# Gated FFN up-projection: the two products that need only token chunk 0 computed ahead of the seven-product loop, and no tile computed classically any more

## The chip, the cores and the metric

One NeuronCore of a Trainium2 chip runs the whole kernel. The metric is the device time of one execution in microseconds (us); the median of several executions is compared. The engines are named as the profile names them: PE (TensorE), PEld (its weight loads), DVE (VectorE), ACT (ScalarE), POOL (GpSimd), SP (SyncE, which issues every DMA here).

## What is computed

Two residual layers over x of shape (1, 1024, 1024) in float32: layer 0 has a mixer of attention and spatial gating, layer 1 a convolution module. After each mixer comes the same gated feed-forward block, and a final norm ends the program. The change touches the feed-forward block only:

```
def conv_ffn(h, w_up, dw_w, dw_b, w_down):
    hh = causal_dwconv(h @ w_up, dw_w, dw_b)      # w_up: 1024 x 5632, conv width 3 along the tokens
    a, gate = jnp.split(hh, 2, axis=-1)           # 2816 channels each
    return (a * jax.nn.silu(gate)) @ w_down

x = x + conv_ffn(rms_norm(x, norm_ffn_g[l]), ffn_w_up[l], ffn_dw_w[l], ffn_dw_b[l], ffn_w_down[l])
```

## The kernel before

**Precision.** Each float32 operand of a matmul is split into a rounded high part and a low rest (`split_hi_lo`: the high part is a cast on ACT, L143, the low part a subtraction on POOL or DVE, L147), and three matmuls replace one (`PASSES`). A matmul here has a 128x128 weight block and 512 columns. The tokens come in two chunks of 512; `hT[0]` and `hT[1]` hold the normalised, transposed and split activations of chunk 0 and 1.

**Up-projection, classical.** The 5632 output channels are 22 gate tiles and 22 value tiles of 128 channels. `head_steps` computes a gate tile and its value tile for one chunk: 2 x 24 matmuls (`chan_mm`, L307), the convolution as one ACT pass (L582) and two DVE passes over 512 columns (L585) with small halo operations (L588, L591), Silu on ACT (L598) and the product on DVE (L602). 3 of the 22 pairs of tiles in layer 0 (`PRE0`) and 8 in layer 1 (`PRE1`) are done so, for chunk 0 and for chunk 1, beside other work that leaves PE gaps: the norms of chunk 1, the depthwise convolution and layer norm of layer 1's mixer, and `combos`.

**Up-projection, seven products.** The other 19 and 14 pairs go through `pair_steps`, a Strassen scheme of Winograd's form: gate and value tile are the two column blocks, the two halves of the 1024 inputs the row blocks, the two chunks the token blocks. Seven products of 12 matmuls (L680) replace eight. Products 1 and 2 use `hT[0]` (chunk 0) alone; 5, 6 and 7 use the combinations T1, T2, T3 (named t or t12 and t3 in the trace) that `combos` makes by loading the normalised rows of both chunks from DRAM (`xnd`, L633), subtracting (L636 to L639) and transposing (L647); 3 and 4 use `hT[1]`, whose lower half `combos` overwrites with a fourth combination. Products 1, 6, 7, 4 accumulate in a PSUM bank A, 5 and 3 in a bank C, 2 in a bank Bk. A is read out three times on the way: after 1 (p1, ACT, L715), after 6 (u2, ACT, L721), after 7 (DVE, L725) and at the end (ACT, L732); C after 5 (p5, ACT, L718) and 3 (DVE, L723); Bk on DVE (L728). The results go to SBUF rows `rg` and `rv_` of 1024 tokens, which the convolution reads in one ACT pass (L686) and two DVE passes (L688) each; L734 multiplies.

The weights of a tile (512 KB each for gate and value) are loaded by SP (L695), and five of their linear combinations are made by L700, L702, L703 (DVE) and L705 (POOL), split by ACT (L143) and by POOL or DVE (L147). In layer 0 the result is split and stored for a classical down-projection (`store_split`). In layer 1 the down-projection has seven products as well, so `finish` combines each couple of pairs j and j + 11 (`sums`: three POOL operations, L554 to L556, one on DVE, L558) and stores them.

**Order.** Program order only sets priorities: a list scheduler orders every engine's queue at build time, and at run time each queue is strictly in order. `interleave(main, shadow, start, end)` spreads one list of steps over another. `keep_in_program_order` (`pin`) holds an instruction at its place. Pools of fixed size limit how far ahead work can run: 4 raw weight tiles (`WRAW`), 8 split halves (`WHL`), 4 rows (`ROWS`), 4 single banks.

Of the kernel before, what the change touches and what calls it, by code (L numbers as in the profile page):

```python
# [58 lines left out]
def trunk_kernel(ctx: ExitStack, tc: tile.TileContext, x, norm_mix_g, norm_ffn_g, ab_w_in, ab_w_out,  # L59
# [515 lines left out]
    def head_steps(l, c, hT, js):  # L575

        dw, halo, w_up = dws[l], halos[l], ffn_w_up[l]

        def up(ct):
            ps = chan_mm(chan_unit(w_up, ct), hT[c])  # L580
            y = s2([P, CH])
            nc.scalar.activation(out=y, in_=ps, func=AF.Identity, scale=dw[:, 2, ct:ct + 1], bias=dw[:, 3, ct:ct + 1])  # L582
            for k in range(2):
                sh = 2 - k
                nc.vector.scalar_tensor_tensor(out=y[:, sh:], in0=ps[:, :CH - sh], scalar=dw[:, k, ct:ct + 1],  # L585
                                               in1=y[:, sh:], op0=ALU.mult, op1=ALU.add)
                if c > 0:
                    nc.vector.scalar_tensor_tensor(out=y[:, :sh], in0=halo[:, ct, k:2], scalar=dw[:, k, ct:ct + 1],  # L588
                                                   in1=y[:, :sh], op0=ALU.mult, op1=ALU.add)
            if c < NCH - 1:  # L590
                nc.vector.tensor_copy(out=halo[:, ct, :], in_=ps[:, CH - 2:])  # L591
            return y

        cur = {}

        def up_g(j):
            cur["g"] = yg = up(HT + j)
            nc.scalar.activation(out=yg, in_=yg, func=AF.Silu)  # L598

        def up_a(j):  # L600
            ya = up(j)
            nc.vector.tensor_tensor(out=ya, in0=ya, in1=cur["g"], op=ALU.mult)  # L602
            if l == 0:
                store_split(ya, s2([P, CH], F32R), j, slice(c * CH, (c + 1) * CH))
            elif c == 0:
                nc.sync.dma_start(out=phs[:, SLOT[1 + j // HH], j % HH, :], in_=ya)
            elif j < HH:
                cur["v"] = ya
            else:
                jj = j - HH  # L610
                old = s4([P, S])
                nc.sync.dma_start(out=old.rearrange("p (i c) -> p i c", i=2), in_=phs[:, 0:3:2, jj, :])
                sums(jj, old[:, :CH], cur["v"], old[:, CH:], ya)
                nc.sync.dma_start(out=phs[:, SLOT[4], jj, :], in_=ya)
                nc.sync.dma_start(out=phs[:, SLOT[7], jj, :], in_=cur["v"])

        return [f for j in js for f in (lambda j=j: up_g(j), lambda j=j: up_a(j))]
# [39 lines left out]
    def pair_steps(l, hT, T, js, up_pool):  # L657
# [12 lines left out]

        def part(raw, lo_eng):
            hl = whl.tile([P, 2, 512], F32R, tag="whl", name="hl")
            split_hi_lo(raw, hl[:, 0, :], hl[:, 1, :], lo_eng=lo_eng)
            return hl.rearrange("p s (d c) -> p s d c", c=P)

        def product(ps, n, hv, start, stop):
            i = 0
            for d in range(4):
                for sw, sa in PASSES:
                    nc.tensor.matmul(ps, lhsT=hv[:, sw, d, :], rhs=B[n](sa, d), start=(start and i == 0),  # L680
                                     stop=(i == 11), skip_group_check=True)
                    i += 1
# [9 lines left out]
        def f(j):  # L692
# [18 lines left out]
            rg, rv_ = row(), row()
            A, C = bank(), bank()
            product(A, 1, a1, True, False)
            p1 = s2([P, CH])
            nc.scalar.copy(out=p1, in_=A)  # L715
            product(C, 5, a5, True, False)
            p5 = s2([P, CH])
            nc.scalar.copy(out=p5, in_=C)  # L718
            product(A, 6, a6, False, False)
# [451 lines left out]
```

## Time and profile before

| | |
|---|---|
| runs | median 2269.41 us of 3 (2268.31 to 2272.55) |
| profiled execution | 2265.38 us, of which the profile's span 2263.6 us |
| PE busy | 2138.7 us, 94% of the span, 9846 matmuls |
| DVE, ACT, POOL busy | 65%, 48%, 40% |
| DMA | 346.58 MB, 16 engines busy 46.3% |

The profile is one execution. Busy time is the union of an engine's instructions; matmuls overlap each other, so the mean duration of one (about 0.39 us) is longer than the distance from one to the next. What a stage costs is read from the distance between equal points of its steps. An idle time and its releaser stand ahead of the instruction that waited.

### The profile page before, as it was taken

To read this page: it belongs to the slowest core of one execution; us is meant where nothing else is said; L and a number is where in the kernel's file an instruction comes from. 1 tells how busy PE (TensorE), PEld (TensorE's weight loads), DVE (VectorE), ACT (ScalarE), POOL (GpSimd) and SP (SyncE) were. 2 spreads that over 40 slices of the span, in tenths; PEclk is the share of its full clock that TensorE was granted. 3 is DMA by queue.
4 is the path that set the end of the run, shared out by engine and by line. 5 is a ranking of instruction groups with operands and counts; after the bars stand their busy time and mean duration, and the time that the engine had idled before them with its cause. 6 is when DMAs were issued, how large, how long until landed. Compare 5 with 4: busy or idle time off the path is not lost. (4 is left out here: it accounts for less than half of the span.)

```text
span 2263.6 us, 28251 instructions
## 1 busy us (share of the span) xinstructions
PE 2138.7 (94%) x9846; PEld 1755.1 (78%) x9846; DVE 1481.1 (65%) x2671; ACT 1092.8 (48%) x1899; POOL 905.1 (40%) x772
## 2 busy tenths in 40 slices
PE   8989999898999999999999979989998999999987
PEld 6768777787788888878788868767777888878876
DVE  5456787458666666600399569996576576756686
ACT  4245665244455555522455474555443454544354
POOL 1222010134344443344489827963544455530011
PEclk9999999999999999999999979989989999999999
DMA  6375433466233333588655723432653223238433
GB/s 226 112 244 172 128 124 134 141 231 197 75 112 105 108 107 109 201 305 286 212 168 168 259 60 100 152 100 93 221 165 127 95 91 117 93 132 319 130 98 107
DMA packets 300495, 346.58 MB, mean 153 GB/s; under 512 B 12988, under 2 KB 207296, under 8 KB 299840
## 3 DMA queue, kind: packets, MB, share of 16 engines
q1 hardware_dynamic: 300352, 344.77, 46.3%
q8 instruction: 78, 1.28, 0.2%
q14 instruction: 65, 0.53, 0.1%
HBM read 261.62 MB, written 83.10 MB: 152 GB/s over the span
## 5 line engine op out<-in xcount | busy, mean ns | idle before, releaser
L147 POOL TENSOR_TENSOR hl<-raw,hl 128x512 fp32r<-128x512 f32 x424 | 570.5, 1364 | 605.4 <-ACT hl L143 511.5
L307 PE MATMUL bank<-big,hl 128*128 128x512 f32 x1824 | 427.7, 394 | 4.1 <-ACT big L223 2.4
L270 PE MATMUL bank<-hl,big 128*128 128x512 f32 x1728 | 422.1, 400 | 7.2 <-ACT big L143 2.8
L143 ACT CAST hl<-raw 128x512 fp32r<-128x512 f32 x476 | 280.0, 618 | 257.5 <-issue 96.9
L307 PEld LDWEIGHTS bank<-big,hl 128*128 128x128 f32 x1824 | 343.2, 189 | 76.6 <-ACT big L223 3.3
L270 PEld LDWEIGHTS bank<-hl,big 128*128 128x128 f32 x1728 | 325.1, 192 | 78.1 <-ACT big L143 3.3
L680 PE MATMUL bank<-big,hl 128*128 128x512 f32 x1584 | 375.3, 390 | 0.3 <-ACT hl L143 0.3
L680 PEld LDWEIGHTS bank<-big,hl 128*128 128x128 f32 x1584 | 297.1, 188 | 64.0 <-ACT hl L143 1.0
L680 PE MATMUL bank<-t,hl 128*128 128x512 f32 x1188 | 290.4, 395 | 6.5 <-ACT hl L143 6.0
L688 DVE SCALAR_TENSOR_TENSOR bank<-row,dw,bank 128x1024 f32<-128x1024 f32 x132 | 169.7, 1286 | 162.8 <-ACT bank L686 161.6
L680 PEld LDWEIGHTS bank<-t,hl 128*128 128x128 f32 x1188 | 224.4, 189 | 57.6 <-ACT hl L143 6.9
L862 PE MATMUL bank<-hl,ph 128*128 128x512 f32 x1056 | 247.9, 395 | 5.3 <-DMA ph<-phd 3.3
L1006 DVE SCALAR_TENSOR_TENSOR sbank<-yb,cw,sbank 128x512 f32<-128x512 f32 x352 | 246.0, 749 | 5.0 <-ACT sbank L995 1.8
L862 PEld LDWEIGHTS bank<-hl,ph 128*128 128x128 f32 x1056 | 199.8, 190 | 49.7 <-DMA ph<-phd 4.3
L824 PE MATMUL bank<-hl 128*128 128x512 f32 x726 | 176.1, 397 | 10.4 <-DVE s L734 4.4
L824 PEld LDWEIGHTS bank<-hl 128*128 128x128 f32 x726 | 138.9, 192 | 42.1 <-ACT hl L143 5.0
L1003 POOL TENSOR_TENSOR ap<-ap,pr 128x512 f32<-128x512 f32 x112 | 147.8, 1319 | 14.2 <-ACT ap L998 10.3
L143 ACT CAST hl<-s 128x512 fp32r<-128x512 f32 x110 | 68.3, 621 | 108.8 <-POOL s L705 50.3
L1002 ACT ACTIVATE pr<-yb,cw 128x512 f32<-128x512 f32 x112 | 80.7, 723 | 63.5 <-POOL ap L1003 62.8
L705 POOL TENSOR_TENSOR s<-raw,s 128x512 f32<-128x512 f32 x33 | 43.6, 1320 | 157.9 <-DVE hl L147 83.5
L1112 POOL TENSOR_TENSOR xr<-xr,gain 128x512 f32<-128x512 f32 x10 | 14.5, 1481 | 201.5 <-ACT xn L1104 176.1
L585 DVE SCALAR_TENSOR_TENSOR s<-bank,dw,s 128x510 f32<-128x510 f32 x88 | 65.5, 745 | 35.8 <-ACT s L582 34.8
(202 smaller groups left out, 2577.3 us busy)
## 6 DMA issues: line engine op xcount, KB each, us to landing
raw<-in_ffn_w_up SPq DMA_DIRECT2D x110, 512.0 KB
ph<-phd SPq DMA_DIRECT2D x88, 512.0 KB
raw<-in_ffn_w_down SPq DMA_DIRECT2D x44, 512.0 KB
phd<-s SPq DMA_DIRECT2D x38, 512.0 KB
ph<-phs SPq DMA_DIRECT2D x33, 512.0 KB
raw<-in_conv_w_in SPq DMA_DIRECT2D x32, 512.0 KB
raw<-in_ab_w_in SPq DMA_DIRECT2D x32, 256.0 KB
qd<-s SPq DMA_DIRECT2D x32, 256.0 KB
```

The source lines that it names most:

```text
L143: nc.scalar.copy(out=hl_hi, in_=raw)
L147: eng.tensor_sub(out=hl_lo, in0=raw, in1=hl_hi.bitcast(F32))
L270: nc.tensor.matmul(ps, lhsT=hT[t // TPC][:, sa, d, tok(t)], rhs=units[d][:, sw, :], start=(n == 0), stop=(n == 3 * DT - 1))
L307: nc.tensor.matmul(ps, lhsT=hv[d // 4][:, sw, d % 4, :], rhs=hT[:, sa, d, :], start=(n == 0), stop=(n == 3 * DT - 1))
L585: nc.vector.scalar_tensor_tensor(out=y[:, sh:], in0=ps[:, :CH - sh], scalar=dw[:, k, ct:ct + 1], in1=y[:, sh:], op0=ALU.mult, op1=ALU.add)
L680: nc.tensor.matmul(ps, lhsT=hv[:, sw, d, :], rhs=B[n](sa, d), start=(start and i == 0), stop=(i == 11), skip_group_check=True)
L688: nc.vector.scalar_tensor_tensor(out=y, in0=r[:, k:k + S], scalar=dw[:, k, ct:ct + 1], in1=y, op0=ALU.mult, op1=ALU.add)
L824: nc.tensor.matmul(ps[k], lhsT=a[:, sa, k * P:(k + 1) * P], rhs=w[:, sw, :], start=(n in (5, 2, 1) and js[0] == 0 and i == 0), stop=(end a ...
L862: nc.tensor.matmul(ps, lhsT=phs[i][:, sa, k * P:(k + 1) * P], rhs=wds[i][:, sw, :], start=(dp == 0 and n == 0), stop=(dp == DP - 1 and n = ...
L1002: nc.scalar.activation(out=pr, in_=ys[ct][:, k:k + CH], func=AF.Copy, scale=cw[:, ct, k:k + 1])
L1003: nc.gpsimd.tensor_add(out=st["ap"], in0=st["ap"], in1=pr)
L1006: nc.vector.scalar_tensor_tensor(out=st["acc"], in0=ys[ct][:, k:k + CH], scalar=cw[:, ct, k:k + 1], in1=st["acc"], op0=ALU.mult, op1=ALU.add)
```

## The change

- `head_steps` and the halo tiles are gone: all 22 pairs of both layers go through `pair_steps`, in which one of 84 matmuls per pair.
- For 9 pairs in layer 0 and 16 in layer 1 ("early" pairs) a new step, `ahead_steps`, computes products 1 and 2 of the gate tile: it loads the gate weights (512 KB), splits both halves, runs 24 matmuls, copies product 1 out on ACT, adds product 2 to it on DVE, and stores both (512 KB) in a DRAM tensor `pcd`. These steps stand where the classical tiles stood: 4 beside the norm of chunk 1 and 5 beside `combos` in layer 0; 9, 3 and 4 in layer 1. In layer 0 the early pairs are 0, 2, ..., 16; in layer 1, whose order is 0, 11, 1, 12, ..., they are 0 to 10 and 11 to 15, so the first ten pairs of the loop are early and then every other one.
- In `pair_steps` an early pair loads p1 and the gate row's chunk 0 from `pcd`, has five products (60 matmuls), and adds p1 on DVE where product 1 was in the accumulation before (p5, u2 and the value row's chunk 0): these three are copies on ACT in a pair that is not early.
- Stores of results go into a list and are issued, pinned, behind the next pair's first loads. `yg` has a buffer of its own instead of one of the three `s4` buffers; `rtc` has 3 buffers instead of 4.

```
-PRE0 = 3
-PRE1, PRE1_LATE = 8, 2
+AHEAD0, AHEAD1 = (4, 5), (9, 3, 4)
...
-    def head_steps(l, c, hT, js):
...
+    def ahead_steps(l, hT, js):
+        def f(j):
+            g = wraw.tile([P, 1024], F32, tag="raw", name="raw")
+            nc.sync.dma_start(out=g.rearrange("p (d c) -> p d c", c=P),
+                              in_=ffn_w_up[l][:, (HT + j) * P:(HT + j + 1) * P].rearrange("(d p) c -> p d c", p=P))
+            pc = s4([P, 2, CH])
+            a1, a2 = part(g[:, :512], "pool"), part(g[:, 512:], "pool")
+            A, B = bank(), bank()
+            product(A, a1, lambda sa, d: hT[0][:, sa, d, :], True, True)
+            nc.scalar.copy(out=pc[:, 0, :], in_=A)
+            product(B, a2, lambda sa, d: hT[0][:, sa, 4 + d, :], True, True)
+            nc.vector.tensor_add(out=pc[:, 1, :], in0=B, in1=pc[:, 0, :])
+            nc.sync.dma_start(out=pcd[:, j, :, :], in_=pc)
+        return [lambda j=j: f(j) for j in js]
...
+            early = j in ahead
+            rg, rv_, p1 = row(), row(), up_pool.tile([P, CH], F32, tag="p1", name="p1", bufs=2)
+            if early:
+                nc.sync.dma_start(out=p1, in_=pcd[:, j, 0, :])
+                nc.sync.dma_start(out=rg[:, 2:2 + CH], in_=pcd[:, j, 1, :])
+            run(stores)
+            stores.clear()
...
+            if not early:
+                product(A, a1, B[1], True, False)
+                nc.scalar.copy(out=p1, in_=A)
+            product(C, a5, B[5], True, False)
+            if early:
+                nc.vector.tensor_add(out=p5, in0=C, in1=p1)
+            else:
+                nc.scalar.copy(out=p5, in_=C)
+            product(A, a6, B[6], early, False)
+            if early:
+                nc.vector.tensor_add(out=u2, in0=A, in1=p1)
+            else:
+                nc.scalar.copy(out=u2, in_=A)
+            product(C, a3, B[3], False, True)
+            nc.vector.tensor_add(out=rg[:, 2 + CH:], in0=C, in1=u2)
             settle()
...
+            product(A, a7, B[7], False, False)
             nc.vector.tensor_add(out=rv_[:, 2 + CH:], in0=A, in1=p5)
...
+            if not early:
+                Bk = bank()
+                product(Bk, a2, B[2], True, True)
+                nc.vector.tensor_add(out=rg[:, 2:2 + CH], in0=Bk, in1=p1)
+            yg = up_pool.tile([P, S], F32, tag="yg", name="yg", bufs=1)
...
+            product(A, a4, B[4], False, True)
+            if early:
+                nc.vector.tensor_add(out=rv_[:, 2:2 + CH], in0=A, in1=p1)
+            else:
+                nc.scalar.copy(out=rv_[:, 2:2 + CH], in_=A)
...
-            interleave(head_steps(l, 1, hT, js[:pre]), first, 0.0, 0.6)
-            run(last)
-            run(pair_steps(l, hT, T, js[pre:], up_pool))
-    ffn_rest(0, hF0, PRE0)
+            interleave(late, first + last, 0.0, 1.0)
+            run(pair_steps(l, hT, T, order(l), ahead, up_pool))
```

**How the queues change.** Line numbers of the changed kernel differ: L584 is its matmul of products, L211 the transposes of a norm, L632 those of `combos`, L667 the weight loads of the loop, L673 and L674 the loads from `pcd`.

Place 1, PE in the middle of layer 1's loop of pairs. A bank's number tells the accumulator; t12_14371 and t12_14372 are T1 and T2 (products 5 and 6), t3 is T3 (product 7), big_12766 is chunk 0 (products 1 and 2) and big_14091 chunk 1 (products 3 and 4). Before, one pair with banks 16384 (A), 16385 (C) and 16454 (Bk):

```order
L680 MATMUL bank_16384<-big_12766,hl_16345 128x512 x12
L680 MATMUL bank_16385<-t12_14371,hl_16349 128x512 x5
L680 MATMUL bank_16231<-big_14091,hl_16224 128x512 x12
L680 MATMUL bank_16385<-t12_14371,hl_16349 128x512 x7
L680 MATMUL bank_16454<-big_12766,hl_16364 128x512 x12
L680 MATMUL bank_16527<-big_12766,hl_16498 128x512 x12
L680 MATMUL bank_16384<-t12_14372,hl_16354 128x512 x12
L680 MATMUL bank_16385<-big_14091,hl_16358 128x512 x12
L680 MATMUL bank_16384<-t3_14373,hl_16361 128x512 x12
L680 MATMUL bank_16528<-t12_14371,hl_16502 128x512 x12
L680 MATMUL bank_16527<-t12_14372,hl_16507 128x512 x12
```

Now, two early pairs with banks 14723/14724 and 14845/14846 (here t12_14207 and t12_14208 are T1 and T2, big_13972 is chunk 1):

```order
L584 MATMUL bank_14724<-t12_14207,hl_14705 128x512 x12
L584 MATMUL bank_14723<-t12_14208,hl_14710 128x512 x12
L584 MATMUL bank_14611<-big_13972,hl_14608 128x512 x12
L584 MATMUL bank_14724<-big_13972,hl_14714 128x512 x12
L584 MATMUL bank_14723<-t3_14209,hl_14717 128x512 x12
L584 MATMUL bank_14723<-big_13972,hl_14720 128x512 x12
L584 MATMUL bank_14846<-t12_14207,hl_14827 128x512 x12
L584 MATMUL bank_14845<-t12_14208,hl_14832 128x512 x12
L584 MATMUL bank_14846<-big_13972,hl_14836 128x512 x12
L584 MATMUL bank_14845<-t3_14209,hl_14839 128x512 x12
L584 MATMUL bank_14958<-t12_14207,hl_14939 128x512 x12
```

A pair has five products instead of seven, and in the first of these two product 4 follows product 7 on bank 14723 with nothing between them; before, two products of the next pair stood between them. This happens in 4 of the ten consecutive early pairs of layer 1, and nowhere in layer 0.

Place 2, PE where layer 0's block begins, behind the last matmuls of the output projection. Before:

```order
L307 MATMUL bank<-big,hl 128x512 x34
L220 MATMUL bank_5156<-ident,xn 128x128 x8
L307 MATMUL bank<-big,hl 128x512 x31
L220 MATMUL bank_5185<-ident,xn 128x128 x8
L307 MATMUL bank<-big,hl 128x512 x37
L220 MATMUL bank_5258<-ident,xn 128x128 x8
L307 MATMUL bank<-big,hl 128x512 x39
```

Now:

```order
L584 MATMUL bank<-big,hl 128x512 x24
L211 MATMUL bank<-ident,xn 128x128 x16
L584 MATMUL bank<-big,hl 128x512 x24
L211 MATMUL bank<-ident,xn 128x128 x8
L584 MATMUL bank<-big,hl 128x512 x24
L211 MATMUL bank<-ident,xn 128x128 x8
L584 MATMUL bank<-big,hl 128x512 x76
```

Between the transposes of the four token tiles of chunk 1 stand fewer matmuls, and the first two tiles' transposes follow each other.

Place 3, SP in layer 1's loop of pairs. Before, from one couple's weight loads to the next:

```order
L695 DMA raw_16636<-in_ffn_w_up 128x8x128
L695 DMA raw_16637<-in_ffn_w_up 128x8x128
L743 DMA phs_101<-s4_16334 128x2x512
L745 DMA phs_101<-s4_16191 128x2x512
L559 DMA phs_101<-sx_16371 128x2x512
L560 DMA phs_101<-s2_16375 128x512
L695 DMA raw_16789<-in_ffn_w_up 128x8x128
```

Now, in the stretch of early pairs:

```order
L667 DMA raw_15161<-in_ffn_w_up 128x8x128
L673 DMA p1_15052<-pcd_101 128x512
L673 DMA p1_15168<-pcd_101 128x512
L559 DMA phs_102<-sx_15000 128x2x512
L674 DMA row_15164<-pcd_101 128x512
L560 DMA phs_102<-s2_15004 128x512
L734 DMA phs_102<-s4_14804 128x2x512
L734 DMA phs_102<-s4_14920 128x2x512
L667 DMA raw_15278<-in_ffn_w_up 128x8x128
```

The loads from `pcd` stand between the weight loads and the stores, and the weights that follow the stores of one couple are those of the second pair of the next couple but one.

## Rows read from the trace of the kernel before

**Rows 1.** The page's busy times: busy us (share of the span) xinstructions.
```profile
PE 2138.7 (94%) x9846; PEld 1755.1 (78%) x9846; DVE 1481.1 (65%) x2671; ACT 1092.8 (48%) x1899; POOL 905.1 (40%) x772
```
**Rows 2.** The page's chain that ended last, by engine, as shares of the span.
```profile
PE 23%; DVE 3%; ACT 1%; issue 0%; POOL 0%; DMA 0%; ACTq 0%; POOLq 0%; DVEq 0%
```
**Rows 3.** Table by stage: us; busy of PE, PEld, DVE, ACT, POOL; clock; DMA share; GB/s.
```profile
505.00:589.00 84.00, 77.98 (x369) 64.34 (x370) 68.53 (x117) 39.00 (x65) 31.40 (x22) 0.96 0.52 167
589.00:958.00 369.00, 367.25 (x1611) 300.37 (x1610) 235.95 (x271) 201.02 (x290) 154.00 (x155) 1.00 0.34 117
...
1466.00:1613.00 147.00, 128.69 (x577) 104.82 (x576) 99.76 (x182) 79.58 (x135) 75.90 (x59) 0.91 0.35 118
1613.00:1750.00 137.00, 127.35 (x591) 105.72 (x589) 104.53 (x162) 57.26 (x94) 68.45 (x54) 0.95 0.52 165
1750.00:2025.00 275.00, 270.44 (x1174) 222.21 (x1175) 184.22 (x190) 131.53 (x198) 139.77 (x127) 0.99 0.33 108
```
**Rows 4.** Groups of matmuls by line over the whole span.
```profile
L307 PE MATMUL bank<-big,hl 128*128 128x512 f32 x1824 | 427.7, 394 | 4.1 <-ACT big L223 2.4 <-DVE xr L541 0.9 <-ACT big L215 0.7
...
L680 PE MATMUL bank<-big,hl 128*128 128x512 f32 x1584 | 375.3, 390 | 0.3 <-ACT hl L143 0.3
...
L680 PE MATMUL bank<-t,hl 128*128 128x512 f32 x1188 | 290.4, 395 | 6.5 <-ACT hl L143 6.0 <-DVE hl L147 0.4
```
**Rows 5.** PE's timeline, layer 0's loop: the same point of two consecutive pairs.
```profile
718.00 5.15 PE L680 MATMUL bank<-big,hl 128*128 128x512 f32 x22
...
737.18 5.15 PE L680 MATMUL bank<-big,hl 128*128 128x512 f32 x22
```
**Rows 6.** Table by stage: one pair of layer 0, two of layer 1.
```profile
718.00:737.18 19.18, 19.18 (x86) 15.77 (x84) 12.12 (x15) 10.57 (x15) 7.74 (x8) 1.00 0.33 110
1890.00:1928.36 38.36, 38.36 (x170) 31.55 (x169) 27.95 (x28) 18.78 (x28) 21.07 (x20) 1.00 0.32 103
```
**Rows 7.** Groups by line in layer 0's loop, four pairs: busy us, mean ns.
```profile
L688 DVE SCALAR_TENSOR_TENSOR bank<-row,dw,bank 128x1024 f32<-128x1024 f32 x17 | 21.8, 1285 | 34.8 <-ACT bank L686 34.6
...
L723 DVE TENSOR_TENSOR row<-bank,s 128x512 f32<-128x512 f32 x4 | 2.7, 679 | 0.0
```
**Rows 8.** DVE's timeline in layer 1's loop: start, us; idle before it in brackets.
```profile
1808.11 0.69 DVE L558 TENSOR_TENSOR s<-s,sx 128x512 f32<-128x512 f32 x1 [4.02 <-POOL sx L556]
...
1809.32 0.68 DVE L700 TENSOR_TENSOR s<-raw 128x512 f32<-128x512 f32 x1
...
1816.97 1.72 DVE L700 TENSOR_TENSOR s<-raw 128x512 f32<-128x512 f32 x1
```
**Rows 9.** DVE's groups of the classical tiles, whole span.
```profile
L585 DVE SCALAR_TENSOR_TENSOR s<-bank,dw,s 128x510 f32<-128x510 f32 x88 | 65.5, 745 | 35.8 <-ACT s L582 34.8
...
L602 DVE TENSOR_TENSOR s<-s,s 128x512 f32<-128x512 f32 x22 | 17.4, 790 | 0.5
```
**Rows 10.** DVE's timeline, layer 0: the norm of chunk 1's first two token tiles.
```profile
508.19 2.08 DVE L196 SCALAR_TENSOR_TENSOR xn<-xr,y,gain 128x1024 f32<-128x1024 f32 x1
...
516.58 1.27 DVE L196 SCALAR_TENSOR_TENSOR xn<-xr,y,gain 128x1024 f32<-128x1024 f32 x1
```
**Rows 11.** SP's timeline, layer 1: first and last store of a normalised tile, a load.
```profile
1620.05 0.34 SPq L239 DMA_DIRECT2D xnd<-xn  x1
...
1647.11 0.34 SPq L239 DMA_DIRECT2D xnd<-xn  x1
...
1649.67 0.33 SPq L633 DMA_DIRECT2D s<-xnd  x1
```
**Rows 12.** DVE's timeline, layer 1: the first use of that load.
```profile
1655.61 0.69 DVE L636 TENSOR_TENSOR xa<-s,xa 128x512 f32<-128x512 f32 x1 [0.48 <-DMA s<-xnd]
```
**Rows 13.** PE's timeline where layer 1's loop begins.
```profile
1754.57 8.13 PE L680 MATMUL bank<-t,hl 128*128 128x512 f32 x24 [6.04 <-ACT hl L143]
```
**Rows 14.** Table by stage: two short stretches with rests of PE.
```profile
1466.00:1488.00 22.00, 6.99 (x35) 5.55 (x33) 21.43 (x28) 12.94 (x18) 15.32 (x11) 0.58 0.41 140
1613.00:1652.00 39.00, 30.83 (x146) 25.56 (x145) 36.74 (x65) 18.43 (x31) 20.05 (x15) 0.85 0.74 232
```

More of the change, by code (lines that the diff above doesn't have):

```diff
@@ L322, in trunk_kernel @@
     phd = dram.tile([P, HT, 2, S], F32, name="phd")
+    pcd = dram.tile([P, HT, 2, CH], F32, name="pcd")
     phs = dram.tile([P, 7, HH, CH], F32, name="phs")
@@ L566, in store_split @@
         for i, part in enumerate((hi, lo)):
-            nc.sync.dma_start(out=phd[:, j, i, cols], in_=part.bitcast(F32))
-    pending = []
+            stores.append(lambda i=i, part=part: pin(nc.sync.dma_start(out=phd[:, j, i, cols], in_=part.bitcast(F32))))
+    pending, stores = [], []
     def settle():
@@ L573, in settle @@
             pending.pop(0)()
-    def head_steps(l, c, hT, js):
[L577 to L617, printed above, removed]
@@ new lines, in part, with product @@
+    def part(raw, lo_eng):
+        hl = whl.tile([P, 2, 512], F32R, tag="whl", name="hl")
+        split_hi_lo(raw, hl[:, 0, :], hl[:, 1, :], lo_eng=lo_eng)
+        return hl.rearrange("p s (d c) -> p s d c", c=P)
+    def product(ps, hv, rhs, start, stop):
+        i = 0
+        for d in range(4):
+            for sw, sa in PASSES:
+                nc.tensor.matmul(ps, lhsT=hv[:, sw, d, :], rhs=rhs(sa, d), start=(start and i == 0),
+                                 stop=(stop and i == 11), skip_group_check=True)
+                i += 1
@@ L669, in row @@
             return r
[L671 to L682, printed above, removed]
         def conv(r, ct):
@@ L707, in f @@
             a7 = part(v1, "pool")
-            a2 = part(g2, "pool")
+            if not early:
+                a2 = part(g2, "pool")
             a4 = part(v2, "pool")
-            settle()
[L711 to L719, printed above, removed]
@@ L731, in f @@
-            product(A, 4, a4, False, True)
-            nc.scalar.copy(out=rv_[:, 2:2 + CH], in_=A)
+            A, C = bank(), bank()
+            p5, u2 = s2([P, CH]), s2([P, CH])
+            if not early:
+                product(A, a1, B[1], True, False)
[5 more added lines that the diff above has]
+                nc.scalar.copy(out=p5, in_=C)
@@ L742, in finish @@
         def finish(jj, ya, yb):
-            nc.sync.dma_start(out=phs[:, 2:4, jj, :], in_=yb.rearrange("p (i c) -> p i c", i=2))
             sums(jj, ya[:, :CH], ya[:, CH:], yb[:, :CH], yb[:, CH:])
-            nc.sync.dma_start(out=phs[:, 0:2, jj, :], in_=ya.rearrange("p (i c) -> p i c", i=2))
+            for i, y in ((0, ya), (2, yb)):
+                stores.append(lambda i=i, y=y: pin(nc.sync.dma_start(out=phs[:, i:i + 2, jj, :],
+                                                                     in_=y.rearrange("p (i c) -> p i c", i=2))))
         pair = {}
@@ L954, in trunk_kernel, with ffn_rest, ahead_of @@
     open_psum(1)
-    interleave(head_steps(0, 0, hF0, order(0)[:PRE0]),
-               norm_steps(1, xtile, norm_ffn_g[0], hF0, spill=(xd[0], xnd)), 0.0, 0.4)
-    def ffn_rest(l, hT, pre):
+    def ffn_rest(l, hT, ahead, late):
         with tc.tile_pool(name=f"up{l}", bufs=1) as up_pool:
             first, last, T = combos(l, hT, up_pool)
-            js = order(l)
-            interleave(head_steps(l, 1, hT, js[:pre]), first, 0.0, 0.6)
-            run(last)
-            run(pair_steps(l, hT, T, js[pre:], up_pool))
-    ffn_rest(0, hF0, PRE0)
+            interleave(late, first + last, 0.0, 1.0)
+            run(pair_steps(l, hT, T, order(l), ahead, up_pool))
+    def ahead_of(l, hT, counts):
+        js = [2 * k for k in range(counts[0] + counts[1])] if l == 0 else order(1)[::2] + order(1)[1::2]
+        js = js[:sum(counts)]
+        steps = ahead_steps(l, hT, js)
+        parts = [steps[sum(counts[:i]):sum(counts[:i + 1])] for i in range(len(counts))]
+        return set(js), parts
+    a0, (mid0, late0) = ahead_of(0, hF0, AHEAD0)
+    interleave(mid0, norm_steps(1, xtile, norm_ffn_g[0], hF0, hb=bank, spill=(xd[0], xnd)), 0.0, 0.8)
+    ffn_rest(0, hF0, a0, late0)
+    run(stores)
+    stores.clear()
     C = ExitStack()
@@ L1127, in trunk_kernel @@
         settle()
+        run(stores)
         run(ds[2:4])
```

36 lines of the change are left out of this document (14 added, 22 removed).

## The prediction, made before the changed kernel was run

> **What bounds the kernel now.** I first read the busy times and the chain that ended last. PE is busy for 94% of the span, and no other engine passes 65% [rows 1]; in the chain, where PE has 23% and the next engine 3%, DMA and issue have none [rows 2]. So a matmul that disappears is time won, as long as the other engines keep up with the shorter queue. The table by stage says where that holds. In layer 0's loop of pairs PE rests 1.8 of 369 us, in layer 1's 4.6 of 275; in the stretches in which the classical tiles stand it rests more: 6.0 us before layer 0's loop, 18.3 and 9.7 us in the two stretches before layer 1's [rows 3]. The reader should see two kinds of stage: loops that PE fills, with DVE at 64% and 67% of the time, and preparations in which classical tiles fill gaps of a chain of other work.
>
> Two equal points of consecutive pairs lie 19.18 us apart [rows 5], which makes 0.2283 us for each of 84 matmuls. All prices of matmuls below use that pace.
>
> **The matmuls that go.** The classical line has 1824 matmuls, the loop 1584 + 1188 = 2772 = 33 x 84 [rows 4]. 768 of the first belong to the convolution module (8 pairs of tiles x 2 x 24 x 2 chunks), so 1056 = 11 x 96 are classical up-projection. They become 11 x 84 = 924: 132 fewer, **-30.1 us** if PE stays full. By place: in layer 0 the preparation has 216 instead of 288 (-16.4 us) and the loop 36 more (+8.2); in layer 1 the preparations have 384 instead of 768 (-87.7) and the loop 288 more (+65.8). The kernel therefore moves work out of the stages with rests into the loops. Everything else in the sum is what the other engines take back.
>
> **Layer 0's loop.** An early pair has 60 matmuls, 13.7 us, the next one 84, 19.2 us: 32.9 us for two. DVE is busy 12.12 us per pair [rows 6]. The early pair adds three additions from PSUM (p5, u2, the value row) and loses one (the gate row comes by DMA); each is a read of one PSUM and one SBUF operand of 512 columns, as L723's 0.679 us [rows 7]. Two pairs thus need 24.2 + 1.4 = 25.6 us of DVE, under 32.9. ACT (10.57 us per pair) loses copies and casts, POOL (7.74) loses two splits per early pair. Priced at 0; the cover is 7 us of DVE per two pairs, and if an early pair waits all the same, one late PSUM read of 0.7 to 1.3 us [rows 7] for each of 9 pairs makes at most 9 to 12. I keep 0 to +9.
>
> **Layer 1's loop, the first ten pairs.** Here all pairs are early, so two pairs need 120 matmuls, 27.4 us of PE. DVE was busy 27.95 us for two pairs [rows 6]; with 2 x 1.36 more it needs 30.7, more than PE. Part of that is stretch: the same operation L700 takes 0.68 us at one time and 1.72 at another [rows 8]. Four or so operations of one pair in two are stretched by 1.0 us; without that, 26.6 us. So DVE needs 26.6 to 30.7 against 27.4, and five couples lose 0 to 16 us. The middle, 28.7, costs 6. Besides, in four of these pairs PE's queue now has product 4 directly behind product 7 on the same bank, and DVE must read the bank between them. That wait is at least one addition (0.68), at most one with a couple of convolution passes of 1.285 before it (3.3) [rows 7]: 2.7 to 13 us; I take 1.0 each, 4, since DVE's queue has that addition near its front. Together **+10** (+3 to +29). DVE may lag about two pairs behind before PE feels it (four banks, four rows), which speaks for the lower half. Behind the tenth pair early and plain pairs alternate, and DVE needs 58.6 us for four against 65.8 of PE: covered.
>
> The row shows the stretch on L700, which reads two SBUF operands, while L723 and L688, with one operand in PSUM, keep 0.68 and 1.29 us [rows 7, 8]. The Trainium skill, page "GPSIMD Engine Reference", section "Specifications", says that GpSimd shares SBUF interfaces with VectorE and contends with its instructions that have two SBUF inputs; the trace agrees with that division. By that rule the three new additions are safe, and the weight combinations are not; that gives the second rival below.
>
> **Layer 0's preparation.** Four norm steps, then the combinations, must pass before the loop can start. The first two xn lie 8.4 us apart [rows 10], and PE's queue now puts 24 matmuls (5.5 us) ahead of both their transposes. PE must rest there for some us, where the old queue had 31 matmuls between them. DVE on the other hand loses the convolution of the classical tiles: per tile and chunk two passes of 0.745, per pair and chunk a product of 0.79 [rows 9], about 3.8 us, of 68.5 busy in this stage [rows 3]; an early step needs one addition of 0.68. So the norms come sooner. I take **+3** (-3: half of the old 6.0 us of rest goes; +10: one more rest of 8.4 and some slow clock).
>
> **Layer 1, convolution and layer norm.** PE loses 72 matmuls (16.4 us), and DVE six such pairs for chunk 0 (6 x 3.8) less nine additions (6.1), 16.7 us. Both shrink alike, so the stage shortens; behind it the layer norm's chain has less filler. **+2** (0 to +8, bounded by the 18.3 us that PE rests there now).
>
> **Layer 1, norm of chunk 1 and combinations.** 168 matmuls (38.4 us) remain of 480. The transposes are what layer 0's stage shows: 78.0 - 288 x 0.2283 = 12.2 us [rows 3]. PE thus has 50.6 us of work. The chain beside it: last xn stored at 1647.11, load issued 2.6 us later, first used 5.9 us after that [rows 11, 12], then four subtractions of about 0.7 and a transpose with its split, some 5 us: 1660.6, or 47.6 us after the stage's start. The stores lie 9.0 us apart (27.06 / 3), and with DVE freed of the classical tiles perhaps 7. So PE is just about the longer one. **+2** (-5: half of the present 9.7 us goes; +12: SP has weight loads that wait for buffers ahead of the chunk-1 loads, two waits of 5.9).
>
> **DMA and SP.** An early pair adds 512 KB three times, weights, store and load: 25 x 1.57 = 39 MB; 11 classical pairs no longer load weights twice, -11.5. In layer 1's loop 108 GB/s [rows 6] over 19.18 us are 2.07 MB per pair; with 0.52 more in 14.4 us it is 180 GB/s, and 232 ran at a share of 0.74 [rows 14]. In SP's queue the weights behind a couple's stores now belong to a pair whose first product lies some 13 products (35.6 us) on, while those stores wait for three POOL operations (DVE's 4.02 us wait in rows 8 is for the same three). That cover of 35.6 us also holds a load of 5.9, so 0.
>
> **Sum.** -30.1 + 10 + 0 + 3 + 2 + 2 = -13.1 against the profiled execution's 2265.4 (span 2263.6): 2252.3. That execution lies 4 us below the median of 2269.4, so for the median **2256**. All lower ends together give -35, all upper ends +38.
>
> **Rivals.**
> - **All of it arrives.** DVE keeps pace because POOL has less to split in early pairs and stretches less. Then -30 or a little less: 2240. For it: PE's rests of only 1.8 and 4.6 us in the loops [rows 3]. Against it: 30.7 of DVE against 27.4.
> - **DVE becomes the bound of layer 1's first ten pairs (slower).** If all ten two-operand operations of a couple are stretched by 1.0, DVE needs 26.6 + 10 = 36.6 us per couple against 27.4: five couples lose 46, and with 7 from the preparations the sum is +23: 2292. It decides from a couple of about 33 us on: 5 x 5.5 + 7 = 34.6, which is the gain and 4.5 more. For it: L700's 1.72, on POOL's busy time of 55% [rows 6, 8]. Against it: POOL has four splits fewer per couple, and only one pair in two was stretched.
> - **The preparations run dry.** PE waits for norms and combinations in both layers, at the upper ends 10 + 8 + 12, and with 4 for the loop: +4, 2273, or with less about 2268, no change. How dear rests are: in a stretch with 15 us of rest the granted clock was 0.58, partly the lower of its levels (1.2 and 2.4 GHz) [rows 14], and after a rest of 6.04 us 24 matmuls took 8.13 us, 0.339 each [rows 13]. The Trainium skill, "TensorE: Matmul & The Clock Gate", Part 1, says that the throttled clock is the default and activity releases it. By it fewer fillers cost twice, the rest and slow matmuls behind it; these rows agree.
>
> That the change does less than it says I exclude: PE's queue shows five products per early pair.
>
> **Chances and range.** The forecast, a gain between 5 and 25 us: 0.52. All of it arrives: 0.18. Preparations dry, near no change: 0.15. DVE the bound, slower: 0.15. About 0.2% of 2269 (4.5 us) is what a measurement can tell from no change. Faster 0.70, same 0.15, slower 0.15. The forecast's own range is 2245 to 2264. With the first rival's 2240 and the third's no change and part of the second, the range is 2240 to 2277.
>
> **What would show it.** PE with 9714 matmuls. In layer 0's loop 32.9 us from one early pair to the next; more means DVE or the banks hold PE. In layer 1's first ten pairs 27.4 us per couple plus the loss; the table by stage would show DVE near 100% there, and the waits "DVE row <- PE" give way to PE waiting for DVE's reads. PE's rests before both loops, near the old ones or a few us more. The forecast is wrong if a couple in layer 1 takes over 33 us, or if rests before the loops grow by more than 20 us in all.

## The result, and the profile after

The changed kernel is slower: 2286.9 us (median of 4 runs, 2286.7 to 2288.5) against 2268.9 (4 runs of the kernel before beside it, 2262.3 to 2272.6); ratio 1.0084, 95% interval 1.0060 to 1.0108. The forecast was 2256, its range ended at 2277. The profiled execution has a span of 2284.6 us, 21.0 more than before.

The page, busy times and the chain that ended last by engine; before in [rows 1, 2]:

```profile
PE 2126.5 (93%) x9714; PEld 1728.8 (76%) x9714; DVE 1550.3 (68%) x2714; ACT 1063.8 (47%) x1825; POOL 874.6 (38%) x772
...
PE 72%; DVE 14%; DMA 5%; ACT 5%; issue 2%; POOL 1%; SPq 0%; ACTq 0%; DVEq 0%; POOLq 0%
```

132 matmuls are gone and PE is busy 12 us less, but it rests 158 us in place of 125. DVE has 14% of the chain, where it had 3%. Where the time came in is read from the table by stage, with the columns of [rows 3]: layer 0's preparation, its loop, and in layer 1 convolution and layer norm, norm and combinations, the loop. About the same points of the program lie in the old kernel at 505.3, 589.0 and 960.8 us, and at 1466.1, 1613.4, 1744.7 and 2025.5, within 6 us of the borders in [rows 3]. Only the border inside layer 0 is not quite the same point: 589.0 is the old loop's first product, while here the first product of the loop starts at 580.9, between transposes that last until 594.65. So layer 0's two stages are read together.

```profile
504.75:594.65 89.90, 76.14 (x360) 62.13 (x361) 52.82 (x96) 31.64 (x59) 25.59 (x24) 0.94 0.54 179
594.65:959.46 364.81, 364.14 (x1594) 298.91 (x1593) 279.72 (x312) 197.76 (x274) 149.43 (x153) 1.00 0.44 146
1465.36:1599.46 134.10, 112.05 (x506) 90.15 (x504) 84.16 (x149) 70.14 (x120) 69.17 (x53) 0.91 0.42 143
1599.46:1657.40 57.94, 51.71 (x245) 41.22 (x244) 46.26 (x79) 24.22 (x42) 23.21 (x17) 0.90 0.70 231
1657.40:2045.00 387.60, 358.88 (x1502) 282.87 (x1501) 301.12 (x333) 159.08 (x219) 171.78 (x170) 0.97 0.42 133
```

Layer 0's two stages together take 454.7 us, as before (455.5). Layer 1's two preparations are 86 us shorter, as forecast, but its loop takes 387.6 us, some 106 more than before, and PE is busy in it for 358.9. All of layer 1, from its first norm's transpose to the first matmul of its down-projection in a main bank, is one row of that view for each kernel. Before:

```profile
1466.13:2033.90 567.77, 530.34 (x2353) 434.84 (x2351) 395.97 (x541) 272.04 (x430) 284.01 (x240) 0.96 0.38 123
```

The changed kernel:

```profile
1465.36:2052.40 587.04, 525.33 (x2258) 415.44 (x2256) 437.59 (x565) 256.23 (x382) 264.22 (x240) 0.95 0.44 144
```

The first experiment (below):

```profile
1468.35:2015.50 547.15, 510.19 (x2258) 414.78 (x2256) 424.38 (x565) 255.47 (x382) 265.07 (x240) 0.96 0.47 154
```

The changed kernel has 96 matmuls fewer here (95 by these records) and takes 19.3 us more. PE's timeline shows how one couple of layer 1's first ten pairs goes (start, us, line, operands, count; idle before it and its releaser in brackets):

```profile
1700.41 2.98 PE L584 MATMUL bank<-big,hl 128*128 128x512 f32 x12 [0.88 <-DVE row L710]
1708.65 1.22 PE L584 MATMUL bank<-t,hl 128*128 128x512 f32 x2 [5.25 <-ACT hl L142]
1710.02 7.43 PE L584 MATMUL bank<-t,hl 128*128 128x512 f32 x22 [0.16 <-DVE hl L146]
1717.29 2.88 PE L584 MATMUL bank<-big,hl 128*128 128x512 f32 x12
1720.01 8.46 PE L584 MATMUL bank<-t,hl 128*128 128x512 f32 x36
...
1737.59 2.96 PE L584 MATMUL bank<-big,hl 128*128 128x512 f32 x12 [0.88 <-DVE row L710]
```

The same couple in the table by stage:

```profile
1700.41:1737.59 37.18, 30.90 (x120) 24.06 (x121) 26.83 (x32) 12.55 (x16) 14.30 (x15) 0.91 0.42 134
```

Equal points are 37.18 us apart, for 120 matmuls that need 27.4 at the pace of [rows 5]. PE waits 0.88 us for DVE's read between products 7 and 4 (L710), then 5.25 us for the cast of product 5's weights (L142), and the 24 matmuls behind that rest come at 0.36 us each. DVE, which is waited for, is itself busy for only 26.83 us of the 37.18. What it did meanwhile (DVE's timeline; the order of the rows is its queue):

```profile
1699.58 0.69 DVE L710 TENSOR_TENSOR row<-bank,s 128x512 f32<-128x512 f32 x1 [0.42 <-PE bank L584]
1700.18 1.22 DVE L723 TENSOR_TENSOR s<-bank,yg 128x1024 f32<-128x1024 f32 x1
1702.68 1.29 DVE L660 SCALAR_TENSOR_TENSOR bank<-row,dw,bank 128x1024 f32<-128x1024 f32 x1 [1.28 <-ACT bank L658]
1703.87 0.69 DVE L719 TENSOR_TENSOR row<-bank,p 128x512 f32<-128x512 f32 x1
1704.47 1.28 DVE L660 SCALAR_TENSOR_TENSOR bank<-row,dw,bank 128x1024 f32<-128x1024 f32 x1
1705.66 0.69 DVE L558 TENSOR_TENSOR s<-s,sx 128x512 f32<-128x512 f32 x1
1706.26 0.69 DVE L680 TENSOR_TENSOR s<-raw 128x512 f32<-128x512 f32 x1
```

L680 makes the weights of product 5 of the couple's second pair. It reads weights that were loaded long before: SP issued the last weight load ahead of it by 1691.8 us, such a load lands within 3.9 us, and none of the 20 L680 from 1670 us to the loop's end waits for a load. Yet it stands behind the product of one pair (L723), the gate's convolution of the next (two L660, with a rest of 1.28 us for ACT's pass ahead of them) and L558, the difference that closes the couple before. [Rows 8] show the same neighbours in the old kernel, L558 and then L700.

### The profile page after: what moved, and what is told of

Same layout as the page of the kernel before. It is cut to its first block, busy times and chain, and to the rows that moved or that the text cites. A ratio compares the mean times of both kernels' runs of the same rounds, so it can differ in the third digit from the quotient of the medians.

```text
span 2284.6 us, 28129 instructions
## 1 busy us (share of the span) xinstructions
PE 2126.5 (93%) x9714; PEld 1728.8 (76%) x9714; DVE 1550.3 (68%) x2714; ACT 1063.8 (47%) x1825; POOL 874.6 (38%) x772
## 4 chain that ended last, share of the span: by engine, by line
PE 72%; DVE 14%; DMA 5%; ACT 5%; issue 2%; POOL 1%; SPq 0%; ACTq 0%; DVEq 0%; POOLq 0%
PE bank L584 33%; PE bank L269 13%; PE bank L852 10%; PE bank L814 5%; PE bank L306 4%; DVE sbank L1002 3%; PE sbank L814 2%; DVE hl L146 2%; DMA ph<-phd 1%; DVE y L180 1%; DVE bank L660 1%; DMA s<-xnd 1%; ACT e L445 1%; PE sbank L211 1%; PE sbank L465 1%
## 5 line engine op out<-in xcount | busy, mean ns | idle before, releaser
L146 POOL TENSOR_TENSOR hl<-raw,hl 128x512 fp32r<-128x512 f32 x380 | 507.8, 1356 | 532.5 <-ACT hl L142 445.0
L584 PE MATMUL bank<-big,hl 128*128 128x512 f32 x2112 | 511.2, 394 | 10.0 <-DVE row L710 6.2
L584 PEld LDWEIGHTS bank<-big,hl 128*128 128x128 f32 x2112 | 397.3, 190 | 99.8 <-DVE row L710 5.0
L584 PE MATMUL bank<-t,hl 128*128 128x512 f32 x1584 | 395.2, 400 | 21.4 <-ACT hl L142 16.4
L584 PEld LDWEIGHTS bank<-t,hl 128*128 128x128 f32 x1584 | 301.1, 191 | 96.7 <-ACT hl L142 20.8
L142 ACT CAST hl<-raw 128x512 fp32r<-128x512 f32 x432 | 252.4, 619 | 234.8 <-issue 96.9
L660 DVE SCALAR_TENSOR_TENSOR bank<-row,dw,bank 128x1024 f32<-128x1024 f32 x176 | 226.2, 1285 | 72.7 <-ACT bank L658 64.0
L306 PE MATMUL bank<-big,hl 128*128 128x512 f32 x768 | 176.7, 390 | 0.8 <-ACT big L214 0.7
L306 PEld LDWEIGHTS bank<-big,hl 128*128 128x128 f32 x768 | 144.0, 188 | 30.9 <-ACT big L214 1.2
L142 ACT CAST hl<-s 128x512 fp32r<-128x512 f32 x143 | 88.4, 618 | 168.1 <-DVE s L683 69.6
L658 ACT ACTIVATE bank<-row,dw 128x1024 f32<-128x1024 f32 x88 | 106.4, 1209 | 98.7 <-DVE s L723 48.1
L685 POOL TENSOR_TENSOR s<-raw,s 128x512 f32<-128x512 f32 x44 | 58.3, 1326 | 188.9 <-DVE hl L146 145.5
```

What stands on the lines that cost most here:

```text
L142: nc.scalar.copy(out=hl_hi, in_=raw)
L146: eng.tensor_sub(out=hl_lo, in0=raw, in1=hl_hi.bitcast(F32))
L306: nc.tensor.matmul(ps, lhsT=hv[d // 4][:, sw, d % 4, :], rhs=hT[:, sa, d, :], start=(n == 0), stop=(n == 3 * DT - 1))
L584: nc.tensor.matmul(ps, lhsT=hv[:, sw, d, :], rhs=rhs(sa, d), start=(start and i == 0), stop=(stop and i == 11), skip_group_check=True)
L658: nc.scalar.activation(out=y, in_=r[:, 2:], func=AF.Identity, scale=dw[:, 2, ct:ct + 1], bias=dw[:, 3, ct:ct + 1])
L660: nc.vector.scalar_tensor_tensor(out=y, in0=r[:, k:k + S], scalar=dw[:, k, ct:ct + 1], in1=y, op0=ALU.mult, op1=ALU.add)
```

## The experiments

Theory A: the place of L680 in DVE's queue. Theory B: DVE has too much to do, stretched by POOL (the prediction's slower rival). Theory C: weights or SP late. In the changed kernel PE's waits in layer 1's loop are 16.8 us for L142, 6.2 for L710 and 4.9 for L146, 27.9 in all. All times beside 2266 to 2268 us of the kernel before on the same chip.

**e1, a buffer of its own.** In program order the tile that L558 writes comes ahead of the next pair's `s`, which L680 writes, and both are from the ring `s2` of five buffers.
```diff
-S2 = 5
+S2 = 4
-        s4_ = s2([P, CH])
+        s4_ = wk.tile([P, CH], F32, tag="sd", name="sd", bufs=1)
```

> Only one buffer changes: the difference that L558 writes once per couple of pairs in layer 1 gets a buffer of its own, and the shared ring of 512-column buffers has 4 places in place of 5, so the bytes are the same. In the changed kernel that ring is handed out in program order, so the weight combination L680 of every second pair stands directly behind L558 in DVE's queue; with the edit it stands some ten operations further ahead. Theory A (place in DVE's queue): layer 1's first ten pairs lose time because an early pair begins with product 5, whose weights come from L680, and L680 stands too far back. Then the rests of PE before product 5 (16.8 + 4.9 us in the loop, their slow matmuls about 8, restarts about 4) go: couples of 28 to 30 us in place of 37.2, about 2255 in all (2245 to 2265). Theory B (DVE has too much to do, stretched by POOL): the work is the same, so the couples stay at 35 to 37 and the time at 2280 to 2290. Theory C (weights or SP late): no load moves, 2280 to 2290 as well.

Measured: 2244.6 us (2241.8 to 2248.0), ratio 0.9901 (0.9876 to 0.9926): 42 us faster than the changed kernel, with the same instructions. PE's timeline, equal points of three neighbouring pairs:

```profile
1687.16 8.46 PE L584 MATMUL bank<-t,hl 128*128 128x512 f32 x36
...
1700.89 8.46 PE L584 MATMUL bank<-t,hl 128*128 128x512 f32 x36
...
1714.62 8.46 PE L584 MATMUL bank<-t,hl 128*128 128x512 f32 x36
```

The table by stage for these two pairs:

```profile
1687.16:1714.62 27.46, 27.46 (x121) 22.54 (x120) 24.98 (x29) 11.27 (x16) 15.17 (x15) 1.00 0.38 114
```

Two pairs in 27.46 us, the clock at its upper level, PE never resting. The 36 matmuls on combinations are product 7 and then 5 and 6 of the next pair, which the scheduler now puts ahead of product 4 of the old one, so the wait for L710 is covered too. In DVE's queue the next pair's L680 stands between the two passes of one convolution, and L558 six places behind it:

```profile
1709.99 0.73 DVE L680 TENSOR_TENSOR s<-raw 128x512 f32<-128x512 f32 x1
1710.65 1.28 DVE L660 SCALAR_TENSOR_TENSOR bank<-row,dw,bank 128x1024 f32<-128x1024 f32 x1
1711.84 0.68 DVE L682 TENSOR_TENSOR raw<-raw 128x512 f32<-128x512 f32 x1
...
1715.34 0.68 DVE L558 TENSOR_TENSOR sd<-s,sx 128x512 f32<-128x512 f32 x1
```

Over the whole loop those waits of 27.9 us are gone; the products wait 1.5 us in all (1.1 for L146 on POOL, 0.4 for L703). Theory A holds; B and C said 2280 or more. The edit does not move L680 alone: with it the scheduler orders all queues anew, and no run moved only L680. That its place is what counts rests on this run together with e7, e5 and e8 below.

**e4, DVE's additions left out.**
```diff
-            if early:
+            if early and l == 0:
                 nc.vector.tensor_add(out=p5, in0=C, in1=p1)
```
and the same for `u2` and the value row; these pairs lack product 1 in their results.

> In layer 1 the early pairs leave out the three additions of p1 on DVE (L698, L703, L719) and copy the banks on ACT as plain pairs do; the results of these pairs lack product 1. DVE does 6 additions less per couple, some 4.1 us. L680 of every second pair still stands directly behind L558. Theory A: the rests before product 5 stay within a third of 16.8 + 4.9 us, 2275 to 2290. Theory B: DVE is the bound, so each couple gives 4 us or more back, first ten pairs 20 us and the others 6: 2255 to 2266.

Measured: 2289.1 us, ratio 1.0092 (1.0065 to 1.0119). With six additions less in the couple (the rows count 25 operations for 32, one of them at the edge of the stretch) and 3.3 us less busy time of DVE, and with the copies on ACT (15.81 us for 12.55), PE still waits for DVE and ACT, 36.18 us per couple (table by stage):

```profile
1702.27:1738.45 36.18, 31.28 (x120) 24.29 (x120) 23.53 (x25) 15.81 (x23) 14.72 (x16) 0.91 0.39 124
```

PE's two waits in it, for the same two operations:

```profile
1702.27 3.02 PE L584 MATMUL bank<-big,hl 128*128 128x512 f32 x12 [1.55 <-DVE row L710]
1708.68 1.22 PE L584 MATMUL bank<-t,hl 128*128 128x512 f32 x2 [3.38 <-ACT hl L142]
```

The couple is 1.0 us shorter, where theory B asked for 4 or more, and PE's waits in the loop for L142, L710 and L146 are 27.8 us as before (15.8, 10.4 and 1.6). The copies load ACT, which also makes the cast that PE waits for, so this run alone would not decide. With e1, where DVE has all of its work and PE does not wait, theory B falls.

**e8, L558 on POOL.**
```diff
-        nc.vector.tensor_sub(out=s4_, in0=a12, in1=s2_)
+        nc.gpsimd.tensor_sub(out=s4_, in0=a12, in1=s2_)
```

> The changed kernel with L558 on POOL in place of DVE, and its buffer in the common ring as it was. Two mechanisms for the late place of L680: (1) L558 waits in DVE's queue for POOL's three sums, and what stands behind it waits too; then the edit gives most of e1's gain, 2245 to 2260. (2) the ring of buffers is handed out in program order, so L680's buffer comes only after that of L558, whichever engine writes it; then L680 keeps its place behind the convolutions and the time stays at 2275 to 2290.

Measured: 2291.7 us, ratio 1.0115 (1.0095 to 1.0134): the second mechanism's time, 1.7 us above its range. L558 has left DVE's queue, but L680 keeps its place behind both passes of that convolution (DVE's timeline):

```profile
1707.95 1.29 DVE L660 SCALAR_TENSOR_TENSOR bank<-row,dw,bank 128x1024 f32<-128x1024 f32 x1 [1.28 <-ACT bank L658]
...
1709.75 1.28 DVE L660 SCALAR_TENSOR_TENSOR bank<-row,dw,bank 128x1024 f32<-128x1024 f32 x1
1710.93 1.58 DVE L680 TENSOR_TENSOR s<-raw 128x512 f32<-128x512 f32 x1
```

POOL's timeline, where L558 now is:

```profile
1710.70 1.26 POOL L558 TENSOR_TENSOR s<-s,sx 128x512 f32<-128x512 f32 x1
```

So it is not that L680 waits behind a waiting L558. With the ring shared, it still starts just behind L558 (0.23 us after the start), though on another engine; with a buffer of its own it does not. That the scheduler hands the ring out in program order is what both runs agree with; its working was not looked at.

**e5, the same edit in the kernel before.**

> The kernel before, with the same one edit as e1 (the buffer of L558 its own, the ring of 512-column buffers 4 in place of 5). Theory A: there every pair begins with product 1, whose weights need no DVE operation, so the late place of the weight combination was covered: nothing is won, 0 to +5 us against the kernel before (the shorter ring may cost a little, since its pairs hold four such buffers). If the edit were worth its 42 us by itself, it would show here as 2225 to 2235.

Measured: 2256.6 us (8 runs), ratio 0.9961 (0.9950 to 0.9973), 9.5 us faster, which theory A had not expected. The old kernel paid once: [rows 13], a rest of 6.04 us and 24 slow matmuls at its loop's first pairs. DVE's timeline there, before:

```profile
1752.57 0.69 DVE L558 TENSOR_TENSOR s<-s,sx 128x512 f32<-128x512 f32 x1 [2.54 <-POOL sx L556]
1753.18 0.68 DVE L700 TENSOR_TENSOR s<-raw 128x512 f32<-128x512 f32 x1
```

And with the edit:

```profile
1741.94 0.68 DVE L700 TENSOR_TENSOR s<-raw 128x512 f32<-128x512 f32 x1
...
1756.22 1.75 DVE L558 TENSOR_TENSOR sd<-s,sx 128x512 f32<-128x512 f32 x1 [2.83 <-POOL sx L556]
```

L700 comes 11 us earlier and the rest is gone. In the later pairs, which ran at PE's pace [rows 5, 6], product 1, which needs no DVE operation, covered the same late place. Against e5 the change brings 12.0 us by the medians (2244.6 to 2256.6), 13.6 by the two ratios.

**e2 and e7, early and plain pairs alternating.** In e2 with the shared ring, in e7 with the buffer of its own.
```diff
-AHEAD0, AHEAD1 = (4, 5), (9, 3, 4)
+AHEAD0, AHEAD1 = (4, 5), (6, 2, 3)
```

(The expectation of e2 speaks of 60 matmuls more; that was a slip. An early pair has 24 + 60, as many as a plain one; 120 matmuls move from the stretches before into the loop.)

> AHEAD1 = (6, 2, 3): layer 1 has 11 early pairs in place of 16, the first of each couple, so that early and plain pairs alternate from the start; 60 matmuls more. Theory A: all eleven couples run as the last six of the changed kernel did, 35.2 us (first ten pairs of the changed kernel: 31.5 to 37.3), loop about 387 us as now although it has 60 matmuls more, and the stretches before it shorten by up to 120 x 0.2283 = 27 us: 2262 in all (2255 to 2272). Theory B: DVE needs 29 to 34 us per couple against 32.9 of PE, couples 33 to 35, 2255 to 2270: the two differ little here. If the stretches before the loop run dry with 5 tiles fewer, 2270 to 2280.

> e1 with AHEAD1 = (6, 2, 3), so e2 with the buffer of its own. Theory A: couples of 32.9 us in place of 35.2, eleven of them, 25 us less than e2: 2255. Against e1 the same number of matmuls per pair and tile in all, but five tiles (27 us of PE) fewer beside norm and combinations: 2255 would put a price of 10 us on the dry preparation.

Measured: e2 2280.1 us, ratio 1.0061 (1.0040 to 1.0083); e7 2261.5, ratio 0.9984 (0.9968 to 0.9999). Equal points of neighbouring couples in PE's timeline, e2:

```profile
1735.18 3.01 PE L584 MATMUL bank<-big,hl 128*128 128x512 f32 x12 [0.55 <-DVE row L710]
...
1770.42 3.02 PE L584 MATMUL bank<-big,hl 128*128 128x512 f32 x12 [0.55 <-DVE row L710]
```

e7:

```profile
1731.84 2.91 PE L584 MATMUL bank<-t,hl 128*128 128x512 f32 x12
...
1764.74 2.91 PE L584 MATMUL bank<-t,hl 128*128 128x512 f32 x12
```

35.24 and 32.90 us, both as expected. Both totals were missed, by 18 and 6.5 us; e2's is what its expectation gave for stretches that run dry. From layer 1's first norm to its last combination e2 takes 193 us and e7 195, against 204 and 205 with five tiles more (the changed kernel, e1). 27 us of PE's work taken out shortened the stretch by 11, so the rest of it was cover for the chain of norms and combinations.

**e3, e6, e9, filler in layer 0.** e3 is the changed kernel with one tile moved; e9 is e1 with two tiles more in layer 0, e6 also has three more in layer 1 (their lines in the order e3, e9, e6).
```diff
-AHEAD0, AHEAD1 = (4, 5), (9, 3, 4)
+AHEAD0, AHEAD1 = (3, 6), (9, 3, 4)
+AHEAD0, AHEAD1 = (5, 6), (9, 3, 4)
+AHEAD0, AHEAD1 = (5, 6), (9, 4, 6)
```

> AHEAD0 = (3, 6): in layer 0 one early tile moves from beside the norm to beside the combinations. In the changed kernel PE rests 5.6 us beside the norm and 8.1 us beside the combinations. Theory: the combinations' rests are a lack of filler there; one tile more (5.5 us) takes 3 to 5 us off them, and costs as much or less beside the norm: 2282 to 2288. If the order of the chain and not the number of tiles makes the rests, no change: 2286 to 2288.

> e1 with AHEAD0 = (5, 6) and AHEAD1 = (9, 4, 6): two early tiles more in layer 0, three more in layer 1 (11 and 19 early pairs); the number of matmuls is the same, 24 per tile move from the loop to the stretch before it. In e1 PE rests 13.7 us in layer 0's preparation and about 20 us in layer 1's norm and combinations. If these rests are a lack of filler, 5 to 12 us go: 2233 to 2240. If the chain of norms and combinations only gets later with more tiles in the queues, 2244 to 2250.

> e1 with AHEAD0 = (5, 6) and AHEAD1 as it was: the half of e6 that paid. In e6 the stretch from layer 0's first early tile to its down-projection took 438.0 us against 448.8 in e1 (PE's rests 4.9 in place of 12 us beside norm and combinations), while layer 1 with its three more tiles took about 3 us longer. If the two halves are independent, 2244.6 - 10.8 = 2234 (2230 to 2240). If e6's gain in layer 0 was a chance of that one execution, 2242 to 2247.

Measured: e3 2292.1 us, ratio 1.0103 (1.0076 to 1.0130), not to be told from the changed kernel; e6 2244.7, ratio 0.9907 (0.9887 to 0.9927), not to be told from e1; e9 2238.7 (2236.2 to 2245.9), ratio 0.9884 (0.9865 to 0.9903), the fastest median, though its interval overlaps e1's. PE's waits in layer 0's preparation (what waited, for what: us in total, times, longest), changed kernel:

```profile
PE sbank L632 <- DVE t L635: 8.1, 6, 3.2
PE bank L211 <- DVE xn L195: 5.6, 1, 5.6
```

e3:

```profile
PE bank L211 <- DVE xn L195: 8.6, 2, 5.6
PE sbank L632 <- DVE t L635: 3.5, 5, 1.6
```

e9:

```profile
PE sbank L632 <- DVE t L635: 4.9, 5, 2.1
```

One tile moved (e3) takes 4.6 us off one rest and adds 3.0 to the other, as its theory said; the time did not fall to 2282 to 2288. From the first early tile to the down-projection layer 0 takes 446.2 us in e3, hardly less than the 446.8 to 449.1 of the six runs with AHEAD0 = (4, 5). Two tiles more (e9) end the rest for xn, put one of 1.0 us in its place, and take 3.2 us off the other: the same stretch takes 439.7 us in e9 and 438.1 in e6, outside that spread. In layer 1, e6's three tiles more brought nothing (550.5 us against 549.9 in e9 and 547.1 in e1).

## Why the prediction was wrong

- **The matmuls.** 9714, 132 fewer: right. Right too where PE fills the time: layer 0's loop runs at 32.90 us per early and plain couple, as forecast, and PE rests 0.7 us in it. That loop has early and plain pairs too, but no L558.
- **Layer 1's preparations.** Forecast -14.4 and about -69 us, measured -13.1 and -73.4: right. That most of what is left there covers a chain was not part of the forecast; e2 and e7 showed it.
- **Layer 0's preparation.** +3 forecast. Layer 0 from its first early tile to the down-projection should have become 5.2 us shorter and became 1.5 shorter (450.6 to 449.1), so the term was about +6.7, inside its bounds; the other five runs with the same tiles give 446.8 to 449.0, or +4.4 to +6.6. The rest of 5.64 us for xn is the one that was named; the other 8.1, for the combinations' splits, were not.
- **Layer 1's loop, the step that failed.** Two terms of the sum were too small, and both lack the same wait, that of PE for product 5's weights: "Layer 1's loop, the first ten pairs", +10 (bounded by +29), and the pairs behind the tenth, "covered", so nothing. Layer 1 should have become 7.9 us shorter and became 19.3 longer, 27 of the 34 us by which the profiled span misses the sum. The table by stage for L584 alone (us; busy of PE and PEld; clock; DMA share; GB/s) shows eight of the first ten pairs and the eleven behind them:

```profile
1682.83:1820.20 137.37, 119.01 (x481) 92.72 (x480) 0.95 0.45 144
1820.21:2016.21 196.00, 187.30 (x792) 148.24 (x791) 0.99 0.37 117
```

At the pace of [rows 5], 480 and 791 matmuls need 109.6 and 180.6 us: 27.8 us were lost in the first stretch, nearly the upper bound, and 15.4 in the second. That is 33 beyond the two terms; the old loop's own loss at its start ([rows 13], a rest of 6.04 and slow matmuls for 2.7) is gone against it, which leaves some 24 of the 27.
- **Why that wait was not seen.** I priced DVE by its amount (26.6 to 30.7 us per couple against 27.4) and took its queue to be in a good order. The amount was no larger than that: 24.98 us in e1, 26.83 here, and one operation stretched in a couple (L680, 1.82 us, at 1718.10). But the change took away the head of the pair. A plain pair begins with product 1, whose weights ACT and POOL split straight from the load, and has product 2 between 7 and 4; the early pair begins with product 5, whose weights are the last thing in DVE's queue. I checked PE's queue for products back to back, and never asked which operation stands at the pair's head and where its producer stands. The rows were there: [rows 8] with L700 right behind L558, and [rows 13], which I read as the price of a rest and not as its cause. "DVE may lag about two pairs behind before PE feels it" did not cover this: the banks and rows that it counts hold results, and PE waited for weights.
- **The wait between 7 and 4.** Foreseen at 1.0 us, measured 0.55 to 0.88; e1 shows that it too goes when the next pair's weights are early.
- **The alternating pairs.** "Covered" was wrong by 2.3 us per couple (35.2 in place of 32.9; the first of these couples lost some 6), for the same reason; e7 has 32.90.
- **The rival "DVE becomes the bound"** gave 2292 and 36.6 us per couple: nearly the time, by another mechanism. Its own sign was missing, DVE near 100%; it was busy for 72% of the couple, and e4 took its work away in vain.
- **What the skill's rule gave.** By the Trainium skill, "GPSIMD Engine Reference", section "Specifications", the additions that read PSUM were safe and the weight combinations not; the trace agrees (the 25 each of L698, L703 and L719 took at most 0.69 us, the 44 of L680 0.68 to 1.82). It decided nothing here.
- **The trade itself.** Beside a kernel before with the same queue order (e5), it is worth 12 to 13.6 us, with 13.1 forecast. That is partly luck, misses that cancel: in the profiled executions layer 1 became 14.5 us shorter from e5 to e1 with 7.9 forecast, because its loop cost next to nothing in place of +10; layer 0 became 1.1 shorter with 5.2 forecast; and e1 took 4.5 us more outside both.

What stays open: how much L680's place would give without the rest of the new order, since no run moved it alone; and why e6's and e9's layer 1 is some 3 us longer than e1's, which may be one execution's chance.

## What to carry to other kernels

When a step is moved away, look at what then stands at the head of the loop's body and follow its producers back through their queues: an engine that is busy for 72% of the time, as DVE here, can still be the one that is waited for. A ring of buffers shared by unrelated values can fix an instruction's place in a queue, as e1 and e8 suggest; if an operation whose inputs are long there runs late, look at what was written to its pool just before it. And when a forecast weighs an engine's amount of work, read its queue's order at one turn of the loop as well.

## What the runs showed of the hardware

A rest of PE and the pace behind it are not tied by that rest's length alone. In the changed kernel the next 22 matmuls took 5.28 us after rests of 1.36 and 0.36 us (granted clock 1.00 over them, the upper level), 6.88 after 3.16 and 0.74 (0.75), and 7.43 after 5.25 and 0.16 (0.69); but in e8 two rests of nearly the same length were followed by 5.28 us at a granted clock of 1.00 and by 6.91 at 0.75 (PE's timeline):

```profile
1746.86 0.73 PE L584 MATMUL bank<-t,hl 128*128 128x512 f32 x2 [1.87 <-ACT hl L142]
1747.96 5.28 PE L584 MATMUL bank<-t,hl 128*128 128x512 f32 x22 [0.36 <-DVE hl L146]
...
1778.86 0.74 PE L584 MATMUL bank<-t,hl 128*128 128x512 f32 x2 [1.85 <-ACT hl L142]
1779.95 6.91 PE L584 MATMUL bank<-t,hl 128*128 128x512 f32 x22 [0.36 <-DVE hl L146]
```
